# One Trainium2 core, a transformer block in split float32: the gate and up weights in seven products that PSUM adds up, in an order written out for three engines

## The chip, the core and the metric

The kernel runs on one core of a Trainium2 chip. The metric is device time in microseconds. Three runs of the kernel before took 774.23 to 774.93 us, median 774.81. The engines are TensorE (PE in the profile, PEld for its weight loads), VectorE (DVE), ScalarE (ACT), GpSimd (POOL) and SyncE (SP), whose queue issues the loads from memory.

## The reference

One layer of a streaming encoder on 512 tokens of width 1024: a mixer of two attention groups, cross-attention into 256 memory tokens, and a feed-forward part (FFN). The change lies in the last:

```
g, u = jnp.split(h @ w_gate_up, 2, axis=-1)
return (jax.nn.silu(g) * u) @ w_down
```

`w_gate_up` is 1024 x 5632 (gate and up, 2816 columns each), `w_down` is 2816 x 1024. All is float32.

## The kernel before, in words

**Split arithmetic.** Each float32 operand is split into a rounded high part (a copy on ACT) and the rest as a low part (a subtraction on DVE); a product of 128 x 128 weights is three matmuls, high by high, high by low, low by high.

**FFN up, in 22 blocks.** The hidden columns come in eleven units u of 256. Block 2u is the gate's 256 columns of a unit, block 2u+1 the up's. The input `h` lies transposed in `bt`: b11, b21 for tokens 0 to 255 (lower and upper half of the 1024 rows), b12, b22 for tokens 256 to 511. The result of a block is 256 columns by 512 tokens. Blocks 0 and 1 (unit 0) are multiplied plainly in L1078-1088, with weights prepared earlier.

A block is a 2 x 2 by 2 x 2 matrix product, and has two forms. In the plain one (`eight`, L1111) it takes eight products of quarters. In the other (`seven`, L1149) it takes seven products by the scheme of Strassen and Winograd, with sums of quarters of the weights (L951-954, four DVE additions of 128 x 512 a block) and sums of quarters of the input, t1 to t4, which are made once (L1129-1144). `product` (L1090) is one such product: 4 x 3 = 12 matmuls of 128 x 256. Blocks 2, 3 and 11 are plain (EIGHT, L970), the other 17 are sevens.

In a seven of the kernel before, the products land in four PSUM banks (tags a, s, t, o) and DVE adds them up: ACT copies the first product to `v` (L1155), then DVE does five additions that read PSUM (L1161, L1162, L1167, L1169, L1171), ACT applies the silu of a gate block (L1176) and DVE multiplies gate by up in an up block (L1181, L1183). `keep` (L1053) splits the hidden unit (L1062 on ACT, L1063 on DVE) or, for units 4 to 9, leaves it for later.

**The weight ring.** `load_raw` (L896) issues a load of 512 KB from SP's queue into one of three raw buffers, two loads a block. A fill (L919-926) copies from a raw buffer or from the sums into `ring_hi` on ACT (L924) and subtracts into `ring_lo` on DVE (L925). A seven has four fills, one of 128 x 512 and three of 128 x 1024. `take` (L1024) fills ahead as far as the slots of the ring are free. The order of the instructions on every engine is set by the framework's scheduler, from the order of the code and its own estimates.

**FFN down.** Twice (two halves of the output columns) eleven units of `w_down`: units 4 to 8 as sevens too (`seven_products`, L1292), with the hidden unit's sums made by `late_seven` (L1211-1226, DVE operations of 128 x 256 to 128 x 1024) and the weights' by L987-1004; the others plainly (`down`, L1272): 24 matmuls of 128 x 512 for all four token tiles. The fills of `w_down` use the same ring (items of the list of `take`).

Of the kernel before, what the change touches and what calls it, by code (L numbers as in the profile page):

```python
# [14 lines left out]
P = 128  # L15
# [21 lines left out]
def hybrid_block_kernel(  # L37
# [624 lines left out]
    with tc.tile_pool(name="cross", bufs=1, reuse_waits="tile") as cp:  # L662
# [231 lines left out]
        raws = [0]  # L894

        def load_raw(w, k0, nkb, c0, ncol):  # L896
            raws[0] += 1
            raw = wp.tile([P, nkb, ncol], F32, tag="raw", name=f"fraw{raws[0]}", bufs=3)
# [15 lines left out]
        items = []  # L914

        def item(at, size, fill):
            items.append((at, at + size, fill))

# [11 lines left out]
        nslot = [0, 0]  # L930

        def single():
            nslot[0] += 1
            return AS_WEIGHTS + 512 * (nslot[0] % 2)

        def double():
            nslot[1] += 1
            return AS_WEIGHTS + 1024 + 1024 * (nslot[1] % 3)

        def seven_weights(n, c0):  # L940
            raw, total = {}, sums[:, n % 2]
            s2, s4, s3, s1 = (total[:, i] for i in range(4))

            def a11():
                raw["lower"] = load_raw(w_gate_up, 0, 4, c0, 256)
                raw["upper"] = load_raw(w_gate_up, 4, 4, c0, 256)
                return raw["lower"][:, :, :P]

            def s2_s4():
                lower, upper = raw["lower"], raw["upper"]  # L950
                dve.tensor_tensor(out=s1, in0=lower[:, :, P:], in1=upper[:, :, P:], op=ALU.add)  # L951
                dve.tensor_tensor(out=s2, in0=s1, in1=lower[:, :, :P], op=ALU.add)
                dve.tensor_tensor(out=s4, in0=s2, in1=upper[:, :, :P], op=ALU.add)
                dve.tensor_tensor(out=s3, in0=lower[:, :, :P], in1=lower[:, :, P:], op=ALU.add)
                return total[:, 0:2]

            two = dict(c=2, k=4, n=P)
            item(at := single(), 512, fill_from(at, dict(k=4, n=P), a11))
            item(at := double(), 1024, fill_from(at, two, s2_s4))
            item(at := double(), 1024, fill_from(at, two, lambda: raw["upper"], "p c k n -> p k c n"))  # L960
            item(at := double(), 1024, fill_from(at, two, lambda: total[:, 2:4]))

        def eight_weights(n, c0):
            for k0 in (0, 4):
                item(
                    at := double(), 1024,
                    fill_from(at, dict(k=4, n=256), lambda k0=k0: load_raw(w_gate_up, k0, 4, c0, 256)),
                )
# [55 lines left out]
        def take(n=1):  # L1024
            first = taken[0]
            taken[0] += n
            while len(ready) < len(items):
                i = len(ready)
                a, b, fill = items[i]
                if any(j >= first and a < items[j][1] and items[j][0] < b for j in range(max(0, i - 8), i)):  # L1030
                    break
                ready.append(fill())
            return ready[first : first + n]

        take(0)
# [3 lines left out]
        gh, gl, gf = [], [], []  # L1039

        def hidden(u):
# [3 lines left out]
            if u < 4 or u == 10:  # L1045
                return U.rearrange("p t b n -> p b t n")
            if u in (4, 8):
                tag, size = {4: ("vm", 4160), 8: ("pt", 2112)}[u]
# [4 lines left out]
        def keep(u, dst):  # L1053
# [13 lines left out]
            for b in range(2):  # L1067
                gh.append(h[:, b])
                gl.append(l[:, b])
# [6 lines left out]

        accs = [(bank("a"), bank("s")) for _ in range(2)]
# [12 lines left out]
        def product(dst, w, b, first=True, last=True, parts=WHOLE):  # L1090
            for k in range(4):
                if k:
                    parts = WHOLE
                pe.matmul(dst, w[0][:, k, :], b[:, 0, k, :], start=first and k == 0, stop=False)  # L1094
                pe.matmul(dst, w[0][:, k, :], b[:, 1, k, :], start=False, stop=False)  # L1095
                for to in parts:
                    pe.matmul(dst[:, to], w[1][:, k, :], b[:, 0, k, to], start=False, stop=last and k == 3)  # L1097

        left, right = slice(0, 256), slice(256, 512)
        b11, b21, b12, b22 = bt[0][:, 0], bt[0][:, 1], bt[1][:, 0], bt[1][:, 1]  # L1100

        def gate_eight(m, acc):
# [333 lines left out]
```

## Time and profile before

| | value |
|---|---|
| median of three runs | 774.81 us |
| span of the profiled execution | 771.6 us |
| PE busy | 755.6 us, 98% of the span |
| DVE busy | 600.3 us, 78% |
| ACT busy | 429.4 us, 56% |
| granted TensorE clock, mean | 0.998 |
| DMA, mean over the span | 104 GB/s |

The span reaches from the first instruction to the last; of the profiled execution the page gives no other time than the span. The median of the runs is 3.2 us above it, which is taken as what lies around the span. A busy PE is a modelled figure, since matmuls overlap; how fast PE goes is better read from the starts of neighbouring matmuls. A name such as ps_a is the PSUM bank group, `fraw` a raw weight buffer, `sums` the sums of quarters, `ring_hi` and `ring_lo` the weight ring, `thi` and `tlo` t1 to t4, `latex`, `latehi`, `latelo` the hidden units that `late_seven` prepares.

### The profile page before, as it was taken

Reading aid. Unit: us, or ns where it says so; the run is one execution under the profiler, and the core shown is the slowest. Engines: PE = TensorE matmul, PEld = TensorE weight load, DVE = VectorE, ACT = ScalarE, POOL = GpSimd, SP = SyncE. Lnnn points to the kernel's source line nnn. Section 1 sums busy time; section 2 is a strip of 40 time slices with the busy share of each in tenths; the row PEclk is TensorE's granted clock in tenths of the full one; section 3 lists DMA queues with packets and bytes.
Section 4 is the critical chain, followed back from the end, with each engine's and each line's share of the span. In section 5 each row is a group of like instructions: output and inputs, shape, how many; then the busy total and the mean of one; then the engine's idle time right before and its main releaser. Section 6 shows DMA issues by size and latency. Waiting matters only on the chain.

```text
span 771.6 us, 12900 instructions
## 1 busy us (share of the span) xinstructions
PE 755.6 (98%) x5012; PEld 677.0 (88%) x5012; DVE 600.3 (78%) x1098; ACT 429.4 (56%) x784; POOL 62.5 (8%) x105
## 2 busy tenths in 40 slices
PE   9999999999999999999999999999999999999996
PEld 9977888887778988877778999999999999898985
DVE  8668889789886688545653779999899998987746
ACT  7558889567874457444553625554444446553421
POOL 1001132100321210000002100000000000000001
PEclk9999999999999999999999999999999999999999
DMA  7522023422313725311340202332433332233312
GB/s 273 139 70 68 28 56 97 123 82 82 109 56 112 267 98 197 120 54 56 131 143 27 83 28 83 110 110 82 138 110 110 110 110 90 102 112 108 106 59 109
DMA packets 60749, 80.05 MB, mean 104 GB/s; under 512 B 2705, under 2 KB 43665, under 8 KB 60689
## 3 DMA queue, kind: packets, MB, share of 16 engines
q1 hardware_dynamic: 59264, 74.49, 29.9%
q0 software_dynamic: 1280, 4.72, 1.7%
q8 instruction: 39, 0.64, 0.3%
q14 instruction: 22, 0.17, 0.1%
q10 hardware_dynamic: 144, 0.02, 0.0%
HBM read 77.13 MB, written 2.10 MB: 103 GB/s over the span
## 4 chain that ended last, share of the span: by engine, by line
PE 79%; DVE 9%; ACT 6%; issue 3%; DMA 2%; POOL 1%; DVEq 0%; POOLq 0%; ACTq 0%
PE ps_a L144 12%; PE ps_a L146 12%; PE ps_a L143 12%; PE ps_a L1094 3%; PE ps_a L1097 3%; PE ps_a L1095 3%; PE ps_s L1097 3%; PE ps_s L1094 3%; PE ps_s L1095 3%; PE ps_s L143 2%; PE ps_s L144 2%; PE ps_s L146 2%; PE ps_t L552 2%; PE ps_o L561 2%; PE ps_s L533 1%
## 5 line engine op out<-in xcount | busy, mean ns | idle before, releaser
L924 ACT CAST ring_hi<-fraw 128x1024 fp32r<-128x1024 f32 (+1 forms) x62 | 57.2, 932 | 61.0 <-DVE fraw L1003 17.0
L126 DVE TENSOR_TENSOR lo<-raw,hi 128x1024 fp32r<-128x1024 f32 x56 | 68.2, 1224 | 20.5 <-ACT hi L125 20.3
L925 DVE TENSOR_TENSOR ring_lo<-fraw,ring_hi 128x1024 fp32r<-128x1024 f32 (+1 forms) x62 | 66.5, 1075 | 17.4 <-ACT ring_hi L924 17.1
L146 PE MATMUL ps_a<-hTh,lo 128*128 128x512 f32 x192 | 76.6, 399 | 0.0
L144 PE MATMUL ps_a<-hTl,hi 128*128 128x512 f32 x192 | 75.9, 395 | 0.0
L143 PE MATMUL ps_a<-hTh,hi 128*128 128x512 f32 x192 | 75.8, 395 | 0.0
L125 ACT CAST hi<-raw 128x1024 fp32r<-128x1024 f32 x56 | 57.8, 1048 | 25.3 <-PE ps_a L144 21.2
L924 ACT CAST ring_hi<-sums 128x1024 fp32r<-128x1024 f32 x34 | 35.7, 1049 | 35.5 <-PE ps_t L1095 10.2
L925 DVE TENSOR_TENSOR ring_lo<-sums,ring_hi 128x1024 fp32r<-128x1024 f32 x34 | 41.4, 1219 | 2.1 <-ACT ring_hi L924 2.1
L144 PEld LDWEIGHTS ps_a<-hTl,hi 128*128 128x128 f32 x192 | 36.1, 188 | 6.4
L146 PEld LDWEIGHTS ps_a<-hTh,lo 128*128 128x128 f32 x192 | 36.1, 188 | 6.3
L143 PEld LDWEIGHTS ps_a<-hTh,hi 128*128 128x128 f32 x192 | 36.2, 188 | 5.7
L547 ACT ACTIVATE p<-p,nm 128x128 f32<-128x128 f32 (+1 forms) x64 | 36.1, 565 | 8.1 <-DVE nm L537 7.2
L1094 PE MATMUL ps_a<-b,ring_hi 128*128 128x256 f32 x140 | 39.1, 279 | 0.0
L1097 PE MATMUL ps_a<-b,ring_lo 128*128 128x256 f32 (+1 forms) x146 | 39.0, 274 | 0.0
L1095 PE MATMUL ps_a<-b,ring_hi 128*128 128x256 f32 x140 | 38.7, 276 | 0.0
L1097 PE MATMUL ps_s<-b,ring_lo 128*128 128x256 f32 x128 | 35.3, 276 | 0.0
L1095 PE MATMUL ps_s<-b,ring_hi 128*128 128x256 f32 x128 | 35.3, 276 | 0.0
L1094 PE MATMUL ps_s<-b,ring_hi 128*128 128x256 f32 x128 | 35.3, 276 | 0.0
L554 ACT CAST pth<-ps_t 128x128 fp32r<-128x128 f32 (+1 forms) x64 | 27.0, 424 | 14.5 <-PE ps_t L552 13.7
L555 DVE TENSOR_TENSOR ptl<-ps_t,pth 128x128 fp32r<-128x128 f32 (+1 forms) x64 | 30.7, 487 | 5.0 <-ACT pth L554 3.8
L552 PE MATMUL ps_t<-ident,p 128*128 128x128 f32 x160 | 28.1, 275 | 1.1 <-DVE p L549 0.8
(552 smaller groups left out, 2630.5 us busy)
## 6 DMA issues: line engine op xcount, KB each, us to landing
raw<-in_dram SPq DMA_DIRECT2D x64, 512.0 KB, 3.7
fraw<-in_dram SPq DMA_DIRECT2D x62, 512.0 KB, 3.5
cb<-in_dram SPq DMA_DIRECT2D x8, 256.0 KB, 2.5
xo<-in_dram POOLq DMA_DIRECT2D x4, 512.0 KB, 7.5
out_dram<-yd SPq DMA_DIRECT2D x8, 256.0 KB, 2.0
rawv<-in_dram SPq DMA_DIRECT2D x3, 520.0 KB, 6.5
xt<-in_dram SPq DMA_DIRECT2D x3, 512.0 KB, 6.6
gb<-in_dram POOLq DMA_DIRECT2D x3, 512.0 KB, 4.4
```

The costliest lines, as they stand in the source:

```text
L125: act.copy(hi[:, j : j + n, :], raw)
L126: dve.tensor_tensor(out=lo[:, j : j + n, :], in0=raw, in1=f32(hi[:, j : j + n, :]), op=ALU.subtract)
L143: pe.matmul(dst, sh, mh, start=first, stop=False)
L144: pe.matmul(dst, sh, ml, start=False, stop=False)
L146: pe.matmul(dst[:, to], sl, mh[:, to], start=False, stop=last)
L547: act.activation(p[:, :n], p[:, :n], AF.Exp, bias=nm, scale=-1.0, accum_out=sm)
L552: pe.transpose(tp[:, k * P : (k + 1) * P], p[:, k * P : (k + 1) * P], ident)
L924: act.copy(h2, v)
L925: dve.tensor_tensor(out=l2, in0=v, in1=f32(h2), op=ALU.subtract)
L1094: pe.matmul(dst, w[0][:, k, :], b[:, 0, k, :], start=first and k == 0, stop=False)
L1095: pe.matmul(dst, w[0][:, k, :], b[:, 1, k, :], start=False, stop=False)
L1097: pe.matmul(dst[:, to], w[1][:, k, :], b[:, 0, k, to], start=False, stop=last and k == 3)
```

## The change

Six things are changed, all in the FFN's gate and up part.

1. **More sevens.** Block 2 alone is plain; blocks 3 to 21, nineteen of them, are sevens.
2. **PSUM adds up.** A block has three banks: `x`, `p45` and `p2`. Product 1 goes into `x`; ACT copies it out to `early[0]`; product 6 is added on top of it in PSUM; ACT copies that to `early[1]`; product 7 is added on top; ACT copies that to `u3`. Products 4 and 5 go into the two halves of `p45`, and product 3 is added on product 5. DVE then needs one addition of 128 x 512 (`op1`: both halves of `p45` plus `u3`, before product 3 is added) and two of 128 x 256 (`op2`).
3. **Order by hand.** From block 3 to 21 the order on PE, DVE and ACT is the order of the code (`own_order`). On PE a block n is p1, p2, p4, p6, p5, then p3 of block n-1, then p7. The last additions of a block (`op2`) and the gate-by-up product come two blocks later.
4. **Raw weights.** `load_block` loads a block's two halves at the start of block n-2, into five places in turn (three raw buffers and two in `more_room`).
5. **t1 to t4** are made before unit 0's matmuls in the code, no longer after.
6. **Into the down part.** Block 21's p3 is issued after the second token tile of the first down unit, and with it the last `op2` and product of unit 10; ring slots that block 21 still reads are `held` against `take`. The hidden units 1 to 3 lie in the large buffer of units 4 to 7.

```diff
-        EIGHT = (2, 3, 11)
-        for n in range(2, FB):
-            (eight_weights if n in EIGHT else seven_weights)(n, (n % 2) * FF + (n // 2) * 256)
+        SEVENS = range(3, FB)
...
+            if places and w is w_gate_up:
+                raw = places[raws[0] % len(places)].rearrange("p (k n) -> p k n", k=nkb)
...
-            product(p17[:, left], a11, b11, parts=parts)
-            act.copy(v, p17[:, left])
...
-            dve.tensor_tensor(out=O[:, 0], in0=halves(p26), in1=twice(v), op=ALU.add)
-            dve.tensor_tensor(out=O[:, 1, 0], in0=p35[:, left], in1=O[:, 0, 1], op=ALU.add)
...
-            dve.tensor_tensor(out=O[:, 1, 1], in0=p17[:, right], in1=O[:, 0, 1], op=ALU.add)
...
-            dve.tensor_tensor(out=O[:, 0, 1], in0=p4[:, left], in1=O[:, 1, 1], op=ALU.add)
...
-            dve.tensor_tensor(out=O[:, 1], in0=twice(p4[:, right]), in1=O[:, 1], op=ALU.add)
...
+            def p6(self):
+                h, l = ring[self.n, "21"]
+                product(self.x[:, left], (h[:, 0], l[:, 0]), t2, first=False, more=True)
...
+            def op1(self):
+                dve.tensor_tensor(out=self.O[:, :, 1], in0=halves(self.p45), in1=twice(self.u3), op=ALU.add)
+
+            def op2(self):
+                dve.tensor_tensor(out=self.O[:, 0, 0], in0=self.p2[:, left], in1=self.early[:, 0], op=ALU.add)
+                dve.tensor_tensor(out=self.O[:, 1, 0], in0=self.p45[:, right], in1=self.early[:, 1], op=ALU.add)
...
+        own_order = tc.manual_schedule(
+            engines={mybir.EngineType.PE, mybir.EngineType.DVE, mybir.EngineType.Activation}
+        )
+        with own_order:
+            for n in SEVENS:
+                final = n == SEVENS[-1]
+                cur = blocks[n] = Seven(n)
+                one, two = blocks.get(n - 1), blocks.get(n - 2)
+                if n + 2 < FB:
+                    load_block(n + 2)
+                if one:
+                    one.copy_u3()
+                if two:
+                    two.op2()
+                    if not two.gate:
+                        two.mult(0)
+                fill_43(n)
+                if two and two.gate:
+                    two.silu(0)
+                cur.p1()
+                cur.copy_early(0)
+                if one:
+                    one.op1()
+                    if not one.gate:
+                        one.mult(1)
+                if two and not two.gate:
+                    keep(two.u, two.dst)
+                if not final:
+                    sums_21(n + 1)
+                    fill_l0(n + 1)
...
+                if one and one.gate:
+                    one.silu(1)
+                cur.p24()
+                if not final:
+                    fill_u(n + 1)
...
+                cur.p6()
+                cur.copy_early(1)
+                cur.p5()
+                if not final:
+                    sums_34(n + 1)
+                    fill_21(n + 1)
+                else:
+                    fill_last(n)
+                if one:
+                    one.p3()
+                cur.p7()
...
+                    if held and t == 1:
+                        cur.p3()
+                        held.clear()
+                        cur.op2()
+                        cur.mult(0)
+                        keep(cur.u, cur.dst)
```

**DVE, one block in the middle.** Before, an up block (its U is the sum, gf the hidden unit), from its first addition:

```order
L1161 TENSOR_TENSOR U<-ps_s_6118,v 128x512
L1162 TENSOR_TENSOR U<-ps_t_6119,U 128x256
L925 TENSOR_TENSOR ring_lo<-fraw_6126,ring_hi 128x4x2x128
L1167 TENSOR_TENSOR U<-ps_s_6117,U 128x256
L1169 TENSOR_TENSOR U<-ps_t_6120,U 128x256
L1171 TENSOR_TENSOR U<-ps_t_6120,U 128x512
L925 TENSOR_TENSOR ring_lo<-sums,ring_hi 128x1024
L1181 TENSOR_TENSOR gf_5664<-G,U 128x512
L1183 SCALAR_TENSOR_TENSOR gf_5664<-G,U 128x512
```

Now the twelve DVE instructions of a whole block n (here n is odd; the first three finish block n-2, an up block, and L1209 is `op1` of block n-1):

```order
L1212 TENSOR_TENSOR U<-ps_a_5631,U 128x256
L1213 TENSOR_TENSOR U<-ps_s_5630,U 128x256
L1220 TENSOR_TENSOR gf_4979<-G,U 128x512
L923 TENSOR_TENSOR ring_lo<-sums,ring_hi 128x1024
L1209 TENSOR_TENSOR G<-ps_s_5744,v 128x2x256
L944 TENSOR_TENSOR sums<-more_room,place_4642 128x512
L945 TENSOR_TENSOR sums<-sums,more_room 128x512
L923 TENSOR_TENSOR ring_lo<-more_room,ring_hi 128x512
L923 TENSOR_TENSOR ring_lo<-place_4642,ring_hi 128x4x2x128
L949 TENSOR_TENSOR sums<-more_room 128x512
L950 TENSOR_TENSOR sums<-sums,place_4642 128x512
L923 TENSOR_TENSOR ring_lo<-sums,ring_hi 128x1024
```

Five additions out of PSUM became three, and the four fills and four sums that stand here are those of the next block (the first fill, of sums 3 and 4, belongs to blocks n and n-1).

**DVE, unit 0, where t1 to t4 are made.** Before (L1139-1142 are the sums of the input, L1125 the product of gate and up of unit 0, L1135 the low parts of the t's), after the second L887, which writes the low part of b22:

```order
L887 TENSOR_TENSOR b_4280<-f_4578,b_4280 128x1024
L953 TENSOR_TENSOR sums<-sums,fraw_4916 128x512
L1139 TENSOR_TENSOR f_4578<-f_4578,f_4577 128x1024
L954 TENSOR_TENSOR sums<-fraw_4914 128x512
L1125 TENSOR_TENSOR G<-G,ps_s_4637 128x512
```

Now, ahead of that same L887 and behind it (L1102 are the first sums of the input, L181 evacuates the transposed input):

```order
L950 TENSOR_TENSOR sums<-sums,fraw_4632 128x512
L1102 TENSOR_TENSOR f_4579<-b_4279 128x1024
L1102 TENSOR_TENSOR f_4580<-b_4279 128x1024
L181 TENSOR_SCALAR f_4578<-ps_t_4599,gn 128x256
L181 TENSOR_SCALAR f_4578<-ps_t_4608,gn 128x256 x2
L887 TENSOR_TENSOR b_4280<-f_4578,b_4280 128x1024
L1103 TENSOR_TENSOR f_4578<-f_4578,f_4577 128x1024
L1104 TENSOR_TENSOR f_4577<-f_4579,f_4577 128x1024
```

The two L1102 (L1138 before) stood behind unit 0's L1125 and now stand ahead of the L887.

**DVE at the end of gate and up, the last block's `op1`** (L1209; L923 from `sums` is the last fill of gate and up, L1302 and L1306-1309 are `late_seven`, L1212 and L1213 are `op2` of block 20):

```order
L923 TENSOR_TENSOR ring_lo<-sums,ring_hi 128x512
L1212 TENSOR_TENSOR G<-ps_a_6848,rrow 128x256
L1307 TENSOR_TENSOR gf_4979<-gf_4979 128x256
L1302 TENSOR_TENSOR latehi<-gf_4979,latehi 128x256
L1213 TENSOR_TENSOR G<-ps_s_6847,rrow 128x256
L1308 TENSOR_TENSOR gf_4979<-gf_4979 128x256
L1302 TENSOR_TENSOR latehi<-gf_4979,latehi 128x512
L1309 TENSOR_TENSOR gf_4979<-gf_4979 128x256
L1306 TENSOR_TENSOR gf_4979<-gf_4979 128x256
L1302 TENSOR_TENSOR latelo<-gf_4979,latelo 128x256
L1307 TENSOR_TENSOR gf_4979<-gf_4979 128x256
L1209 TENSOR_TENSOR U<-ps_s_6956,v 128x2x256
```

Before, the same place, the last additions of block 21:

```order
L1167 TENSOR_TENSOR U<-ps_s_7032,U 128x256
L925 TENSOR_TENSOR ring_lo<-fraw_7162,ring_hi 128x1024
L1169 TENSOR_TENSOR U<-ps_t_7035,U 128x256
L1223 TENSOR_TENSOR gf_5664<-gf_5664 128x256
L1171 TENSOR_TENSOR U<-ps_t_7035,U 128x512
L925 TENSOR_TENSOR ring_lo<-fraw_7154,ring_hi 128x1024
L1181 TENSOR_TENSOR U<-G,U 128x2x256
L1183 SCALAR_TENSOR_TENSOR U<-G,U 128x2x256
```

Now `late_seven` begins inside block 21, and PE's p3 of block 21 stands behind twelve matmuls of the down part and waits for the L1209 at the end of the first list.

More of the change, by code (lines that the diff above doesn't have):

```diff
@@ L928, in fill_from @@
             return fill
[L930 to L961, printed above, removed]
@@ L975, in hybrid_block_kernel, with fill_eight, item @@
+        def fill_eight(n):
+            for k0, at in ((0, AT_21), (1, AT_43)):
+                ring[n, k0] = fill_from(at, dict(k=4, n=256), lambda: raw_of[n][k0])()
+        SEVENS = range(3, FB)
+        items, held = [], []
+        def item(at, size, fill):
+            items.append((at, at + size, fill))
         SEVEN = (4, 5, 6, 7, 8)
@@ L1088, in hybrid_block_kernel, with product @@
                         )
-        def product(dst, w, b, first=True, last=True, parts=WHOLE):
+        def product(dst, w, b, first=True, last=True, parts=WHOLE, more=False):
             for k in range(4):
```

217 lines of the change are left out of this document (132 added, 85 removed).

## The prediction

> **What bounds the kernel now.** I read the page's busy line first, then the table of windows over the FFN, PE's waits, and PE's timeline. The window rows give the stretch, its length, and busy time with instruction count for PE, PEld, DVE, ACT and POOL, then PE's clock, DMA's share and GB/s. 442 to 649 us is gate and up; 680 to 690 is a piece of the down part.
>
> ```profile
> span 771.6 us, 12900 instructions
> PE 755.6 (98%) x5012; PEld 677.0 (88%) x5012; DVE 600.3 (78%) x1098; ACT 429.4 (56%) x784; POOL 62.5 (8%) x105
> 442.00:649.00 207.00, 207.00 (x1824) 206.92 (x1823) 190.95 (x270) 99.50 (x148) 0.00 (x0) 1.00 0.31 98
> 680.00:690.00 10.00, 8.95 (x76) 8.56 (x75) 8.97 (x16) 5.22 (x7) 0.00 (x0) 1.00 0.18 58
> ```
>
> In gate and up PE is never idle, at a granted clock of 1.00. DVE is 92% busy there, but nothing waits for it. So time in this stage is a number of matmuls times PE's pace. In the down part PE has small holes. PE's timeline gives the pace and the holes (start, duration, and in brackets the idle time before it and what ended it):
>
> ```profile
> 469.81 0.28 PE L1094 MATMUL ps_s<-b,ring_hi 128*128 128x256 f32 x1
> 475.48 0.28 PE L1097 MATMUL ps_s<-b,ring_lo 128*128 128x256 f32 x1
> 667.78 0.39 PE L146 MATMUL ps_a<-ring_hi,g 128*128 128x512 f32 x1
> 670.50 0.39 PE L146 MATMUL ps_o<-ring_hi,g 128*128 128x512 f32 x1
> ```
>
> The first two rows lie 50 matmuls apart: 5.67 / 50 = 0.1134 us for 256 columns. The last two lie 12 apart: 2.72 / 12 = 0.2267 us for 512 columns. A product of 12 matmuls takes 1.36 us, a seven 7 x 1.36 = 9.53 us, and a pair of sevens (gate and up) 19.06 us.
>
> ```profile
> 648.94 0.40 PE L143 MATMUL ps_a<-ring_hi,g 128*128 128x512 f32 x1
> 682.42 0.28 PE L143 MATMUL ps_s<-ring_hi,latehi 128*128 128x256 f32 x1
> 683.10 0.38 PE L144 MATMUL ps_s<-ring_lo,latehi 128*128 128x256 f32 x1 [0.41 <-DVE ring_lo L925]
> 683.32 0.28 PE L146 MATMUL ps_s<-ring_hi,latehi 128*128 128x256 f32 x1
> 687.87 0.28 PE L143 MATMUL ps_s<-ring_hi,latelo 128*128 128x256 f32 x1
> 688.79 0.39 PE L144 MATMUL ps_s<-ring_lo,latelo 128*128 128x256 f32 x1 [0.65 <-DVE ring_lo L925]
> 689.02 0.28 PE L146 MATMUL ps_s<-ring_hi,latelo 128*128 128x256 f32 x1
> 681.82 1.22 DVE L925 TENSOR_TENSOR ring_lo<-fraw,ring_hi 128x1024 fp32r<-128x1024 f32 x1
> 687.51 1.23 DVE L925 TENSOR_TENSOR ring_lo<-fraw,ring_hi 128x1024 fp32r<-128x1024 f32 x1
> ```
>
> 648.94 is the first matmul of the down part. Twice in it PE waits for the low half of a weight slot, until DVE's L925 ends (681.82 + 1.22 = 683.04, and 688.74). By starts, the two holes cost (0.90 - 0.227) + (1.15 - 0.227) = 1.60 us; by the modelled idle times 0.41 + 0.65 = 1.06 us. I take the starts, which do not use modelled ends.
>
> **The change part by part.** The sum is made on the profiled execution, whose span is 771.6 us; the median of the runs lies 3.2 us above it, which stays.
>
> *Fewer matmuls.* Blocks 3 and 11 become sevens: 84 matmuls for 96 each. In PE's order there are 24 fewer matmuls of 128 x 256, and the number of stepped ones is the same. 24 x 0.1134 = **-2.72 us**, all of it on the path, since PE sets the pace there.
>
> *Does the written-out order hold PE's pace?* That hangs on DVE first. Its rows, as neighbours, give the start-to-start time for each width:
>
> ```profile
> 597.11 0.69 DVE L925 TENSOR_TENSOR ring_lo<-fraw,ring_hi 128x512 fp32r<-128x512 f32 x1
> 597.71 0.69 DVE L951 TENSOR_TENSOR sums<-fraw,fraw 128x512 f32<-128x512 f32 x1
> 599.51 1.22 DVE L925 TENSOR_TENSOR ring_lo<-sums,ring_hi 128x1024 fp32r<-128x1024 f32 x1
> 600.65 0.69 DVE L1161 TENSOR_TENSOR G<-ps_a,v 128x512 f32<-128x512 f32 x1
> 601.85 0.42 DVE L1162 TENSOR_TENSOR G<-ps_a,G 128x256 f32<-128x256 f32 x1
> 602.18 1.22 DVE L925 TENSOR_TENSOR ring_lo<-fraw,ring_hi 128x1024 fp32r<-128x1024 f32 x1
> 588.52 0.69 DVE L952 TENSOR_TENSOR sums<-sums,fraw 128x512 f32<-128x512 f32 x1
> 589.25 0.69 DVE L953 TENSOR_TENSOR sums<-sums,fraw 128x512 f32<-128x512 f32 x1
> 585.18 0.62 ACT L924 CAST ring_hi<-fraw 128x512 fp32r<-128x512 f32 x1 [0.24 <-DMA fraw<-in_dram]
> 586.33 0.35 ACT L1155 COPY v<-ps_s 128x256 f32<-128x256 f32 x1
> 586.58 1.05 ACT L924 CAST ring_hi<-sums 128x1024 fp32r<-128x1024 f32 x1
> fraw<-in_dram SPq DMA_DIRECT2D x62, 512.0 KB, 3.5
> ```
>
> 0.60 us for 512 columns, 1.14 for 1024, 0.33 for 256; an addition that needs the one before it takes 0.73 in place of 0.60. A pair of blocks before had six operations of 256 (1.98), sixteen of 512 (9.60), six of 1024 (6.84), and some 0.5 of dependence: 18.9 us. Now it has four of 256 (1.32), fourteen of 512 (two `op1`, eight sums, two fills, two multiplies; 8.40), the six of 1024 and the 0.5: 17.1 us. Against PE's 19.06 DVE has 2 us over in a pair; where `keep` stands in the pair (1.14), 0.9.
>
> A sum is not an order, so I set one block of 9.53 us down by hand, with p1 from 0, p2 from 1.36, p4 2.72, p6 4.08, p5 5.45, p3 of the block before 6.81, p7 8.17. On ACT: `copy_u3` 0.1 to 0.4, `fill_43` (1024) to 1.35, silu to 2.0, `copy_early` of p1 to 2.35. p6 needs that at 4.08: 1.7 us of margin. `copy_early` of p6 waits behind `fill_u`, which starts when p4 has left its slot (4.1), and ends near 5.9; p7 needs it at 8.17. On DVE: low part of `fill_43` 1.4 to 2.55 (p3 needs it at 6.81), `op1` to 3.15 (p3 too), then the sums, `fill_l0`, `fill_u`, two more sums and the low part of `fill_21` to 9.3 at the latest; that one waits for p5 to leave its slot and is needed by p6 4 us into the next block. `op2` ends about 0.4 into the next block; the bank that it frees is needed by p4 at 2.7, a margin of 2, or 1.2 behind a `keep`. No margin is below 1 us; cost in the steady blocks **0**. The raw loads are issued two blocks, 19 us, ahead and land in 3.5 us (last row): 0. The first one into `more_room` goes once unit 0 has left it, near 456, and lands near 461, 4 us ahead of need.
>
> On the three products in one bank, the Trainium skill speaks against this change: "Perfetto Trace Analysis", section Matmuls, says that independent matmul groups should rotate through PSUM banks so that the evacuation of one overlaps the next group. Here product 6 may not start before ACT has copied product 1 out of its bank; by the rule that copy would stand uncovered, and by the rows above it is 0.35 us long with two products (2.72 us) of other banks ahead of product 6. The rival "uncovered copies" below prices it.
>
> *Unit 0, ahead of the blocks.* The low parts of the input's second half (L887, b12 and then b22) are what PE just finds ready:
>
> ```profile
> 439.29 0.48 DVE L181 TENSOR_SCALAR f<-ps_t,gn 128x256 f32<-128x256 f32 x1 [1.42 <-ACT b L179]
> 440.41 0.87 DVE L181 TENSOR_SCALAR f<-ps_t,gn 128x256 f32<-128x256 f32 x2
> 442.86 1.22 DVE L887 TENSOR_TENSOR b<-f,b 128x1024 fp32r<-128x1024 f32 x1
> 444.12 0.38 PE L144 MATMUL ps_a<-b,gate_w 128*128 128x256 f32 x1
> 446.40 1.22 DVE L887 TENSOR_TENSOR b<-f,b 128x1024 fp32r<-128x1024 f32 x1
> 447.76 0.40 PE L144 MATMUL ps_a<-b,gate_w 128*128 128x256 f32 x2
> ```
>
> b12: L887 ends at 444.08 and PE's L144 reads it at 444.12. In PE's new order 15 matmuls that stood ahead of that L144 no longer do: 444.1 - 1.7 = 442.4. On DVE the four L181 now stand in a row; from 439.29, at 0.4 each, and L887: 442.1. b22: L887 ended at 447.62, and the second of the two L144 at 447.76 reads it. In PE's new order 19 more matmuls stand ahead of that one: 447.9 + 2.2 = 450.1. On DVE, behind b12's L887 (its successor can start at 442.0), stand four sums of 512, four L181, two L1102 of 1024 and L887: 442.0 + 2.4 + 1.6 + 2.3 + 1.2 = 449.5. Margins of 0.3 and 0.6 us are thinner than I can work out. Bounds: 0, and one operation of 1024 late, +1.1. I take **+0.2**, near the lower end, since both lists end in time. The t1 to t4 made there come long before block 3 needs one.
>
> *The end of gate and up.* Product 3 of block 21 now stands behind twelve matmuls of 512 columns (2.72 us), 12.25 us after its block's start, and waits for `op1` of block 21. Ahead of that `op1` stand nine DVE operations of 256 columns and one of 512 (9 x 0.33 + 0.60 = 3.6 us) that start near 8.15: the last fill waits until p5 leaves its slot at 6.81, then ACT takes 0.62 and DVE 0.69 for it. 8.15 + 3.6 + 0.69 for `op1` itself is 12.45, 0.2 late. Bounds 0, if the additions that need no late result go ahead of that fill, and +0.8, with one more operation of 512; I take **+0.2**.
>
> *The two holes of the down part.* There DVE is late. From 648.94 to the end of the L925 that ends the first hole DVE took 34.1 us. Now `late_seven` begins inside block 21, where DVE has no next block to prepare. From that `op1`, which starts 2.2 us after the last p7, to the same fill stand 27 operations of 256 columns, 13 of 512 and 11 of 1024: 27 x 0.335 + 13 x 0.60 + 11 x 1.135 = 29.3, so 31.5 us. PE reaches the matmul at 33.7 (682.65, where it would have started without the hole, less 648.94) plus the 1.36 of p3, which moved there: 35.1. The lead is 3.6 us, about 2 if DVE waits for ACT on the way, and by the same count a little more at the second hole. Both go: **-1.6**. Bounds: 0, if some wait holds DVE up by over 3 us, and -1.6. Nothing else was late behind these holes.
>
> Sum: -2.72 - 1.60 + 0.2 + 0.2 = -3.9; 774.8 - 3.9 = **770.9 us**, of which the span is 767.7.
>
> **The rivals.** Under 0.2%, 1.55 us, no measurement of this kernel can be told from no change, so faster means below 773.26 and slower above 776.36.
>
> *Forecast*, 0.62: matmuls and holes. Its own range is 770.5 to 772.4: nothing at the two seams, or +0.8 at one and +1.1 at the other.
>
> *Only the matmuls*, 0.15: the holes stay, or move to another fill, since ring slots are held for block 21 and the order of `late_seven` differs. 774.8 - 2.72 = 772.1. For it: my count leaves out DVE's waits for ACT. Against it: a lead of 2 to 4 us.
>
> *New waits at both seams, and the holes stay*, 0.13: -2.72 + 1.1 (L887 late by one operation of 1024) + 0.5 at block 21 (between its 0.2 and its 0.8) = -1.1, 773.7, within 0.2%. For it: margins of 0.3 and 0.6 us and an `op1` that is late by my own count. Against it: it needs all three at once.
>
> *The written-out order paces the blocks*, 0.10 with its extreme, and slower. Its place is DVE's chain: `fill_43` waits for p7 to leave its slot, and all that stands behind it (`op1`, sums, three fills) waits with it. It decides once DVE needs over 19.06 us a pair, 12% above my 17.1. Then PE waits in every pair; at 0.6 us, one operation of 512, 9.5 pairs are +5.7: 774.8 - 2.72 + 5.7 = 777.8, with the holes staying. For it: DVE is the busiest engine after PE. Against it: each margin in the hand-made block is over 1 us. The extreme is *uncovered copies*, 0.02 of the 0.10: two of 0.35 us in each of 19 blocks are +13.3, 785.4. That the blocks are not what the code says can be excluded: PE's order has the 24 fewer.
>
> **How the numbers follow.** The likeliest case gives 770.9. The range goes from 769.8 (the forecast without seam costs is 770.5; 0.7 below it, half a product, for margins worked out from rows of two decimals over a whole stage) to 774.4 (new waits at both seams at their upper ends: 774.8 - 2.72 + 1.1 + 0.8 is 774.0, and 0.4 over it). It leaves out the slower case and some of the rest. Faster 0.62 + 0.15 = 0.77, same 0.13, slower 0.10.
>
> **What the profile after would show.** 24 fewer matmuls; PE without a wait between 455 and the last p7, and starts at 0.1134: right on the steady blocks. PE waiting at p6 or p7 for ACT, or at p4 or p3 for DVE, in every pair: the slower rival. PE idle near 450 before a matmul that reads b22, ended by L887: the first seam; p3 of block 21 ended by L1209: the second. In the down part no wait of PE for L923 at the two seven matmuls with `latehi` and `latelo`: the holes are gone. I am wrong if PE's busy stretch in gate and up is not shorter, or if holes of over 1 us appear there.

## The result, and the profile after

| | before | after |
|---|---|---|
| median of the runs side by side | 774.87 us | 769.96 us (769.24 to 770.32) |
| medians of a second set, in which before stood twice | 774.76 us (21 runs) and 774.42 us (11 runs) | 769.31 us (5 runs) |
| span of the profiled execution | 771.6 us | 767.5 us |
| time of that execution | 771.6 + 1.74 = 773.3 us | 769.24 us |

The changed kernel is faster: ratio 0.9926, 95% interval 0.9906 to 0.9945, in the second set 0.9923 (0.9911 to 0.9936). That ratio is 5.7 us of 774.8, where 3.9 was forecast. It is not the quotient of the two medians: these lie 4.9 us apart in the first set and 5.5 in the second (774.76 less 769.31). Every run comes with its span and lies 1.7 to 1.8 us above it, in both kernels; so the execution of before that the first profile shows took 773.3 us, less than any of the runs that were listed beside it. From profile to profile the change is 4.1 us, close to the forecast's 3.9. The experiments below ask what other executions of the kernel before lose beyond that. In 51 runs beside the experiments it took 773.06 to 776.65 us; the changed kernel's nine took 768.93 to 770.32.

From the page of the changed kernel, and its window over the piece of the down part:

```profile
span 767.5 us, 12862 instructions
PE 752.7 (98%) x4988; PEld 674.4 (88%) x4988; DVE 595.7 (78%) x1083; ACT 442.9 (58%) x811; POOL 63.6 (8%) x105
680.00:690.00 10.00, 10.00 (x91) 10.00 (x90) 8.14 (x12) 5.11 (x6) 0.00 (x0) 1.00 0.44 143
```

There are 5012 - 4988 = 24 fewer matmuls. In 680 to 690 PE has 91 where it had 76, and no idle time. PE's timeline, before: first matmul of unit 0, first of the down part (648.94, in the prediction), last of all.

```profile
427.68 0.28 PE L143 MATMUL ps_a<-b,gate_w 128*128 128x256 f32 x1
764.12 0.28 PE L146 MATMUL ps_a<-ring_hi,g 128*128 128x256 f32 x1
```

After, the same, with the seams and the places of the two holes:

```profile
427.99 0.28 PE L143 MATMUL ps_a<-b,gate_w 128*128 128x256 f32 x1
438.61 0.88 PE L170 MATMUL ps_t<-ident,y 128*128 128x128 f32 x6 [0.17 <-DVE y L161]
441.36 1.06 PE L170 MATMUL ps_t<-ident,y 128*128 128x128 f32 x8 [0.15 <-DVE f L181]
450.86 0.28 PE L1128 MATMUL ps_a<-b,ring_hi 128*128 128x256 f32 x1
451.07 0.38 PE L144 MATMUL ps_a<-b,gate_w 128*128 128x256 f32 x1
645.33 0.40 PE L143 MATMUL ps_a<-ring_hi,g 128*128 128x512 f32 x1
647.85 0.39 PE L146 MATMUL ps_a<-ring_hi,g 128*128 128x512 f32 x1
648.07 0.28 PE L1127 MATMUL ps_s<-b,ring_hi 128*128 128x256 f32 x1
680.19 0.28 PE L143 MATMUL ps_s<-ring_hi,latehi 128*128 128x256 f32 x1
680.30 0.28 PE L144 MATMUL ps_s<-ring_lo,latehi 128*128 128x256 f32 x1
685.06 0.28 PE L144 MATMUL ps_s<-ring_lo,latelo 128*128 128x256 f32 x1
759.99 0.28 PE L146 MATMUL ps_a<-ring_hi,g 128*128 128x256 f32 x1
```

The DVE rows that these wait for, or would:

```profile
441.64 1.23 DVE L887 TENSOR_TENSOR b<-f,b 128x1024 fp32r<-128x1024 f32 x1
449.79 1.22 DVE L887 TENSOR_TENSOR b<-f,b 128x1024 fp32r<-128x1024 f32 x1
647.19 0.68 DVE L1209 TENSOR_TENSOR U<-ps_s,v 128x512 f32<-128x512 f32 x1
677.26 1.22 DVE L923 TENSOR_TENSOR ring_lo<-fraw,ring_hi 128x1024 fp32r<-128x1024 f32 x1
682.25 1.23 DVE L923 TENSOR_TENSOR ring_lo<-fraw,ring_hi 128x1024 fp32r<-128x1024 f32 x1
```

Gate and up, from the first row to the down part: 221.26 us before, 217.34 after, -3.92. Product 3 of block 21 has left it (1.36) and two products are gone (2.72): -4.08, so 0.16 us was lost. The b22 seam is in it: L887 ends at 451.01, 450.86 to 451.07 is 0.21 where 0.11 is the pace, and the step behind it is 0.22 (to 451.29): 0.2 us. The two runs of transposes wait 0.17 and 0.15 for DVE. Product 3 starts at 648.07, one step behind the matmul ahead of it: `op1` had ended at 647.87. At the first hole the fill ends at 678.48, 1.8 us ahead of the matmul at 680.30; at the second 683.48, 1.6 ahead.

The down part, from its first matmul to the last, takes 114.66 us with product 3 in it, 113.30 without, against 115.18 before: -1.88. So the two stages gained 4.4 us and not 4.1: their first row stands 0.3 us later in the profile after, and that start differs from execution to execution (427.57 us in a second profile of before, 428.44 in no_own_order below).

### The profile page after: what moved, and what is told of

Same layout as the page of the kernel before. It is cut to its first block, busy times and chain, and to the rows that moved or that the text cites. A ratio compares the mean times of both kernels' runs of the same rounds, so it can differ in the third digit from the quotient of the medians.

```text
span 767.5 us, 12862 instructions
## 1 busy us (share of the span) xinstructions
PE 752.7 (98%) x4988; PEld 674.4 (88%) x4988; DVE 595.7 (78%) x1083; ACT 442.9 (58%) x811; POOL 63.6 (8%) x105
## 4 chain that ended last, share of the span: by engine, by line
PE 87%; ACT 6%; DVE 4%; issue 2%; POOL 1%; DMA 1%; DVEq 0%; POOLq 0%; ACTq 0%
PE ps_a L144 13%; PE ps_a L146 13%; PE ps_a L143 13%; PE ps_t L1130 3%; PE ps_t L1127 3%; PE ps_s L1128 3%; PE ps_t L1128 3%; PE ps_s L1127 3%; PE ps_s L1130 3%; PE ps_s L143 2%; PE ps_s L146 2%; PE ps_s L144 2%; PE ps_t L552 2%; PE ps_o L561 2%; PE ps_s L533 1%
## 5 line engine op out<-in xcount | busy, mean ns | idle before, releaser
L923 DVE TENSOR_TENSOR ring_lo<-sums,ring_hi 128x1024 fp32r<-128x1024 f32 (+1 forms) x39 | 46.7, 1196 | 12.9 <-ACT ring_hi L922 8.5
L922 ACT CAST ring_hi<-sums 128x1024 fp32r<-128x1024 f32 (+1 forms) x39 | 40.1, 1029 | 17.2 <-PE ps_s L1128 15.6
L922 ACT CAST ring_hi<-fraw 128x1024 fp32r<-128x1024 f32 (+1 forms) x26 | 26.7, 1033 | 33.5 <-DVE fraw L1009 13.9
L923 DVE TENSOR_TENSOR ring_lo<-fraw,ring_hi 128x1024 fp32r<-128x1024 f32 (+1 forms) x26 | 31.0, 1201 | 14.2 <-ACT ring_hi L922 14.0
L549 DVE TENSOR_SCALAR p<-p,rc 128x128 f32<-128x128 f32 (+1 forms) x64 | 26.8, 418 | 0.1
L552 PEld LDWEIGHTS ps_t<-ident,p 128*128 128x128 f32 x160 | 19.3, 140 | 7.3 <-issue 2.4
L143 PE MATMUL ps_a<-hi,oh 128*128 128x512 f32 x64 | 25.5, 399 | 0.0
L1130 PE MATMUL ps_a<-b,ring_lo 128*128 128x256 f32 (+1 forms) x93 | 25.5, 276 | 0.0
L1127 PE MATMUL ps_a<-b,ring_hi 128*128 128x256 f32 x92 | 25.5, 277 | 0.0
L1128 PE MATMUL ps_a<-b,ring_hi 128*128 128x256 f32 x92 | 25.4, 276 | 0.0
```

Of the source, the lines that this page charges most:

```text
L143: pe.matmul(dst, sh, mh, start=first, stop=False)
L552: pe.transpose(tp[:, k * P : (k + 1) * P], p[:, k * P : (k + 1) * P], ident)
L922: act.copy(h2, v)
L923: dve.tensor_tensor(out=l2, in0=v, in1=f32(h2), op=ALU.subtract)
```

## The experiments

Theory A at the start: the gain is the matmuls and the two holes, and all beyond is spread. Theory B: before loses something that its first profile does not show.

### The two kernels again

Both unchanged, in more rounds, each with a new profile.

> The kernel before, unchanged, with a profile of its own. Theory A (the gain is the 24 matmuls, 2.72 us, and the two holes of the down part, 1.6 us; all beyond 4.3 us is spread between executions): ratio 1.000, every run 1.7 to 1.8 us above its span (not 3.2), two waits of PE for the low half of a weight slot near 683 and 689 us again, 1.4 to 1.6 us by starts. Theory B (before loses more than the first profile shows): the holes, or another wait of PE, come to over 2.5 us in this execution.

> The changed kernel, unchanged, in more rounds. Theory A: 4.3 us under the kernel before, ratio 0.9945, and PE without a wait behind 442 us. Theory B: 5 to 6 us under it, ratio 0.9926 or 0.993 as in the first runs.

Measured: 774.42 us, ratio 0.999 (0.9981 to 1.0), and 769.31, 0.9923 (0.9911 to 0.9936). The second profile of before has a span of 772.4 and what the first had not, a wait of PE in the middle of gate and up. PE's timeline there:

```profile
628.14 0.38 PE L1094 MATMUL ps_s<-tlo,ring_hi 128*128 128x256 f32 x1 [1.27 <-ACT v L1155]
```

ACT's timeline at that place:

```profile
626.59 0.62 ACT L924 CAST ring_hi<-fraw 128x512 fp32r<-128x512 f32 x1 [1.28 <-DMA fraw<-in_dram]
627.11 0.72 ACT L1176 ACTIVATE G<-G 128x256 f32<-128x256 f32 x2
627.73 0.35 ACT L1155 COPY v<-ps_s 128x256 f32<-128x256 f32 x1
```

ACT stands 1.28 us in front of a raw load that has not landed. Behind it in ACT's queue are the silus and then the copy of product 1 to `v`, and PE may not write product 7 into that bank before the copy has read it. In the first profile the same load kept ACT waiting 1.00 us, and PE went on without a wait. With this wait and the two holes the second profile loses 2.9 us by starts, where theory B asked for over 2.5: theory B holds for before. From here on the theories are L, late loads, and D, a DVE that is late by itself.

### The matmuls in the old way

```
-        EIGHT = (2, 3, 11)
+        EIGHT = (2, 3)     # sevens18
+        EIGHT = (2,)       # sevens19
```

> The kernel before with block 11 as a seven, nothing else. Theory A: 12 matmuls of 0.1134 us less, 1.36 us, ratio 0.9982; the holes of the down part stay as they are. Theory B (the sevens alone bring the gain): over 2 us less.

> The kernel before with blocks 3 and 11 as sevens: the change's matmuls in the old way of adding up. Theory A: 24 matmuls less, 2.72 us, if t1 to t4, which are made late here, are ready for block 3; up to 1.5 us of that lost if they are not (a wait of PE near 467 us for the t's); holes stay. Theory B: the five additions out of PSUM make DVE the bound (18.9 us of work in a pair of 19.06) once there is no plain block to catch up in: little gain or a loss, with PE waiting for DVE in the sevens.

Measured: 775.02 us, ratio 1.0003 (0.9994 to 1.0013), and 778.42, 1.0044 (1.0029 to 1.0058). With 12 matmuls less nothing is won, which fits neither theory; with 24 less the kernel is slower, the loss that theory B allowed for. ACT's waits for loads from 465 to 650 us (total, times, longest), one row each from before, before_again, sevens18 and sevens19:

```profile
ACT ring_hi L924 <- DMA fraw<-in_dram: 8.1, 6, 2.7
```
```profile
ACT ring_hi L924 <- DMA fraw<-in_dram: 14.7, 8, 3.9
```
```profile
ACT ring_hi L924 <- DMA fraw<-in_dram: 18.8, 9, 4.9
```
```profile
ACT ring_hi L924 <- DMA fraw<-in_dram: 31.0, 11, 5.6
```

The fewer matmuls PE has, the longer ACT waits for loads in these four. In sevens18 PE waits four times for the copy to `v`, 2.2 us; in sevens19 also for low halves (1.8 us) and for t's at block 3 (0.5).

### Five raw buffers, and three

The change's five buffers in the kernel before, alone and with the sevens:

```
+            if places and w is w_gate_up:
+                raw = places[raws[0] % len(places)].rearrange("p (k n) -> p k n", k=nkb)
...
         keep(0, hidden(0))
+        places += [wp.tile([P, 1024], F32, tag="raw", name=f"place{i}", bufs=3) for i in range(3)]
+        more_room = cp.tile([P, 2176], F32, tag="up", name="more_room")
+        places += [more_room[:, i * 1024 : (i + 1) * 1024] for i in range(2)]
```

> The kernel before, with only the change's five raw buffers (three and two in the place of unit 0's up weights) for the loads of gate and up. Theory L (the time that the kernel before loses from one execution to the next is raw loads that land late: ACT's copy out of a raw buffer waits for them, and the copy of v stands behind it in ACT's queue, on which PE's product in the same bank waits): ACT's waits for loads in gate and up fall from 8 to 15 us to under 3, PE waits for no copy of v, 1 to 1.5 us less (ratio 0.998 to 0.9985) and a smaller spread. Theory D (DVE with 18.9 us of work in 19.06 is late by itself): no change, 774.7.

> The kernel before with the five raw buffers and block 11 as a seven (block 3 stays plain, so no product waits for a late t). If DVE's five additions out of PSUM leave room for it: 1.36 us under five_raw, near 770.8. If they don't: PE waits for low halves of weight slots behind block 11, and the time stays at 772 or over, so that the change's three additions are what lets the matmuls count.

> The kernel before with blocks 3 and 11 as sevens and the five raw buffers, adding up by DVE as before. Theory L: the loss of sevens19 goes, 771 to 772 us (774.7 less 1.4 for the loads less 2.7 for the matmuls, plus about 1 for t's that block 3 waits for). Theory D: stays near 778, PE waiting for DVE's low halves.

Measured: five_raw 772.17 us, ratio 0.9964 (0.9949 to 0.9978); sevens18_five 770.22, 0.9952 (0.9938 to 0.9965); sevens19_five 774.19, 0.9992 (0.9983 to 1.0001). Five buffers alone bring 2.8 us, where theory L had expected 1 to 1.5. ACT's waits for loads fall from 8.1 to 2.0 us, and both holes of the down part are gone. The longer of ACT's two remaining waits in five_raw, 465 to 650 us (the other is 0.2):

```profile
ACT ring_hi L927 <- DMA place<-in_dram: 1.8, 1, 1.8
```

From its DVE and PE timelines, the fill at the end of gate and up, the down part's first matmul, the fill at the place of the first hole, the matmul that reads it, and the last matmul:

```profile
648.62 1.23 DVE L928 TENSOR_TENSOR ring_lo<-fraw,ring_hi 128x1024 fp32r<-128x1024 f32 x1
648.94 0.40 PE L143 MATMUL ps_a<-ring_hi,g 128*128 128x512 f32 x1
679.96 1.22 DVE L928 TENSOR_TENSOR ring_lo<-fraw,ring_hi 128x1024 fp32r<-128x1024 f32 x1
682.52 0.28 PE L144 MATMUL ps_s<-ring_lo,latehi 128*128 128x256 f32 x1
762.22 0.28 PE L146 MATMUL ps_a<-ring_hi,g 128*128 128x256 f32 x1
```

Before, the same fill at the end of gate and up, ACT's part and DVE's:

```profile
649.38 2.00 ACT L924 CAST ring_hi<-fraw 128x1024 fp32r<-128x1024 f32 x2 [2.03 <-DMA fraw<-in_dram]
650.47 1.23 DVE L925 TENSOR_TENSOR ring_lo<-fraw,ring_hi 128x1024 fp32r<-128x1024 f32 x1 [1.43 <-ACT ring_hi L924]
```

A late load held ACT, ACT held DVE for 1.43 us, and DVE carried that to the holes 33 us later. With five buffers the same fill starts 1.85 us earlier, and so does the fill at the first hole: 679.96 against 681.82, 1.86 us. It ends 1.3 us ahead of PE's matmul. The down part takes 762.22 - 648.94 = 113.28 us against 115.18: the holes cost 1.90.

With the buffers, block 11 as a seven is worth what its matmuls say: sevens18_five ends gate and up 1.27 us sooner than five_raw (219.75 us against 221.02 from the first matmul of unit 0). So DVE's five additions left room for that, and theory D falls for it. Block 3 does not pay in the old order, and 774.19 is the number of neither theory: PE waits 0.85 us there for t's, then for low halves, and a hole stands in the down part again. How much of that is the t's and how much DVE, these runs don't part.

In the changed kernel, three buffers in place of five, in two ways:

```
-        places += [more_room[:, i * 1024 : (i + 1) * 1024] for i in range(2)]   # three_raw and three_raw_late
...
-                if n + 2 < FB:
-                    load_block(n + 2)
+                if n + 1 < FB:                                                   # three_raw_late
+                    load_block(n + 1)
```

> The changed kernel with three raw buffers in place of five. Theory L: the loads land late again, ACT waits for them in every block and PE behind it: 3 to 15 us more, 772 to 784. Theory D (what carries is the lighter DVE): within 0.5 us of the changed kernel, 769.3 to 769.8.

> The changed kernel with three raw buffers, each block's loads issued one block ahead. The second load of a block can go when the last sum of the block before has read its buffer, about 8 us into the block before that, and lands 3.5 us later, 2 us into a block; ACT's fill wants it at 2.4, DVE's first sum at 3.2. If the five buffers are needed in the new order too: waits of ACT for loads, 1 to 5 us more, 770.5 to 774. If the new order reads late enough: within 0.5 us, 769.3 to 769.8, with hardly a wait of PE.

three_raw writes the loads two blocks ahead into buffers whose contents are still to be read, so part of its blocks work with the weights of a later block; its 770.27 us (0.9936, 0.9923 to 0.9949) says little on lateness. three_raw_late reads the right weights in every block: 769.42, ratio 0.9941 (0.9929 to 0.9954) beside runs of before with a median of 774.37, and its trace ends where the changed kernel's does:

```profile
760.00 0.28 PE L146 MATMUL ps_a<-ring_hi,g 128*128 128x256 f32 x1
```

ACT waits for no load there between 465 and 650 us. So three buffers do in the new order; the old order needed the two more. That it is the later reading and the earlier freeing of the buffers that makes the difference, and not the lighter DVE, is the likely reason and was not tested apart.

### Without the written-out order

```
-        with own_order:
+        if True:
```

> The changed kernel without the written-out order: the scheduler orders the same instructions from block 3 to 21. If the written-out order is part of the gain: 2 to 8 us more, with waits of PE for ACT's copies between the products of one bank. If the lighter DVE and the early loads do it: within 1 us of the changed kernel.

Measured: 770.0 us, ratio 0.9935 (0.9922 to 0.9948), PE without a wait in the blocks. The scheduler put PE's matmuls of the blocks in the same order as the written-out one; what changed is the order on DVE and ACT. By the medians that order is worth 0.7 us at the most, and the intervals of the two ratios overlap. What another order on PE would cost, this run does not show.

### Filling DVE up

```
+            for _ in range(2):                            # dve_plus1; range(3) in dve_plus2
-            dve.tensor_tensor(out=s1, in0=lower[:, :, P:], in1=upper[:, :, P:], op=ALU.add)
+                dve.tensor_tensor(out=s1, in0=lower[:, :, P:], in1=upper[:, :, P:], op=ALU.add)
...
-                parts = IN_STEP if self.gate and self.u in (2, 4, 6, 8, 10) else WHOLE
+                parts = IN_STEP if self.gate and self.u in (2, 4, 6, 8, 10) or self.n in (9, 10, 11) else WHOLE  # plus1_step
```

> The changed kernel with the first sum of each block (128 x 512 on DVE) made twice. By the prediction's count DVE goes from 17.1 to 18.3 us in a pair of 19.06: no wait of PE in the blocks, within 0.4 us of the changed kernel (769.3 in the runs so far), up to 1 us more only in the pairs with keep. If DVE is the hidden bound: 5 us more or over.

> The same sum made three times: 19.5 us in a pair of 19.06, 20.6 where keep stands. By the count PE now waits for DVE in every pair, 0.4 to 1.5 us, 4 to 8 us more in all, 773 to 777. If DVE had more room than counted: no change.

> dve_plus1 with the stepped product (its first low matmul in two halves) also in blocks 9, 10 and 11. Theory S (a wait of 0.06 us of PE in block 8 put its matmuls to 0.1178 us each in place of 0.1133, until the next stepped product 40 us later in block 12): the slow stretch ends at block 9, 521 us, about 1.2 us less than dve_plus1, so 1.2 us nearer to the changed kernel, less 0.06 for each step. Rival (the pace is slower because DVE is busy without a pause there): 0.1178 goes on through blocks 9 to 11, and the time stays that of dve_plus1.

Measured: dve_plus1 771.66 us, ratio 0.9962 (0.9947 to 0.9977); dve_plus2 780.7, 1.0083 (1.0067 to 1.0098); plus1_step 770.65, 0.9957 (0.9945 to 0.997). The threshold lies near where the count put it: dve_plus1, 0.8 us under it in a pair, has no wait of over 0.1 us in the blocks. Above it the price is higher than expected: dve_plus2 loses 11.4 us against the changed kernel, where 4 to 8 stood. In dve_plus2 PE waits at product 4 for `op2`, in its place in the prediction's rival (PE, then DVE):

```profile
537.24 0.28 PE L1131 MATMUL ps_a<-b,ring_lo 128*128 128x256 f32 x1
538.83 0.39 PE L1128 MATMUL ps_s<-tlo,ring_hi 128*128 128x256 f32 x1 [1.31 <-DVE G L1214]
538.36 0.41 DVE L1214 TENSOR_TENSOR G<-ps_s,rrow 128x256 f32<-128x256 f32 x1
```

dve_plus1 is 2.3 us slower all the same, where 0.4, or 1 with the pairs that hold `keep`, was expected. The windows 513 to 555, of dve_plus1, the changed kernel and plus1_step:

```profile
513.00:555.00 42.00, 42.00 (x360) 42.00 (x359) 41.30 (x59) 23.52 (x37) 0.00 (x0) 1.00 0.39 122
```
```profile
513.00:555.00 42.00, 42.00 (x373) 42.00 (x372) 39.15 (x54) 24.10 (x38) 0.00 (x0) 1.00 0.37 118
```
```profile
513.00:555.00 42.00, 41.94 (x369) 41.74 (x368) 41.55 (x59) 23.34 (x37) 0.00 (x0) 1.00 0.39 124
```

In dve_plus1 PE is busy throughout, but gets through 360 instructions in place of 373: 13 x 0.1134 = 1.5 us. (Another 0.3 is a wait at product 3 of block 21; the rest of the 2.3 was not traced.) Where the slower stretch begins in dve_plus1, PE's and DVE's timelines:

```profile
515.07 0.33 PE L1128 MATMUL ps_s<-tlo,ring_hi 128*128 128x256 f32 x1
515.24 0.28 PE L1129 MATMUL ps_s<-tlo,ring_hi 128*128 128x256 f32 x1
547.04 0.28 PE L1129 MATMUL ps_t<-thi,ring_hi 128*128 128x256 f32 x1
514.55 0.41 DVE L1214 TENSOR_TENSOR G<-ps_s,rrow 128x256 f32<-128x256 f32 x1
```

`op2` ends at 514.96, and product 4 starts at 515.07 with one step of 0.17 in place of 0.11. From there PE goes at 0.1178 us a matmul (515.24 to 547.04 are 270 of them) until the stepped product of block 12.

plus1_step was meant to end that stretch at block 9. By the medians it is 1.0 us faster than dve_plus1, where 1.2 was expected, but it does not show that the steps did it. The same place in its trace, product 4 of block 8 and the first of the added steps:

```profile
514.82 0.28 PE L1129 MATMUL ps_s<-tlo,ring_hi 128*128 128x256 f32 x1
521.75 0.33 PE L1131 MATMUL ps_t<-b,ring_lo 128*128 128x128 f32 x2
```

These are 61 matmuls apart, 6.93 / 61 = 0.1136 us: behind a wait of 0.05 us this execution kept the faster pace, before any added step was reached. So the run leaves open whether a step ends the slower pace; in dve_plus1 it did end at one, that of block 12. What the run does show is that a busy DVE does not make the slower pace: DVE is busy for 41.55 of the 42 us here, and PE gets through 369 instructions (three of them added halves).

### The copies bare

```
+                cur.p6()
+                cur.copy_early(1)
                 cur.p24()
...
-                cur.p6()
-                cur.copy_early(1)
                 cur.p5()
```

> The changed kernel with product 6 right behind product 1 in the same bank, ahead of products 2 and 4, so that ACT's copy between them has no matmuls to lie under. The prediction priced an uncovered copy at 0.35 us; ACT's queue has a fill and in half of the blocks a silu ahead of it, so 0.4 to 1.0 us in each of 19 blocks: 8 to 19 us more, 777 to 788. Against that: if the copy costs PE nothing either way (another cause covers it), 769 to 770.

Measured: 792.14 us, ratio 1.0228 (1.0213 to 1.0243), 22.8 more than the changed kernel, above the expected 8 to 19. PE, and ACT below it, in one of the 19 blocks:

```profile
562.32 0.39 PE L1127 MATMUL ps_t<-thi,ring_hi 128*128 128x256 f32 x1 [0.71 <-ACT rrow L1184]
560.42 1.06 ACT L922 CAST ring_hi<-sums 128x1024 fp32r<-128x1024 f32 x1
561.38 0.63 ACT L1216 ACTIVATE G<-G 128x512 f32<-128x512 f32 x1
561.90 0.36 ACT L1184 COPY rrow<-ps_t 128x256 f32<-128x256 f32 x1
```

The 19 places take 0.62 to 1.25 us over the pace by starts. In the two places where ACT is free when product 1 ends, it is 0.62: the copy itself, and the last matmul of product 1, which it waits for. In 8 gate blocks, as here, the silu stands ahead of the copy in ACT's queue, 0.88 or 1.00 us in all. In 9 up blocks the copy waits 0.66 us for DVE, whose product of gate and up (L1220) still reads the half of U that it overwrites; these are the dearest, at 1.25 us, and their wait is no matter of the bank. Here the bank rule of the Trainium skill ("Perfetto Trace Analysis", section Matmuls) is seen at work: with the next group in the same bank, the copy is not covered. In the change products 2 and 4, in other banks, cover it.

### Product 3 of block 21 at its place

```
             cur.op1()
+            cur.p3()
             cur.mult(1)
```

(and its call in the down part taken out).

> The changed kernel with product 3 of the last block at the end of gate and up, no longer behind the first two token tiles of the down part. op1 of that block ended 2.5 us after the last product 7 in the changed kernel: PE waits for it, 2.0 to 2.6 us more, 771.3 to 772. If DVE runs the late op1 earlier there: under 1 us.

Measured: 769.8 us, ratio 0.9938 (0.9922 to 0.9955). The edit did not do what it was for: PE still has ten matmuls of the down part ahead of product 3.

```profile
645.86 0.40 PE L143 MATMUL ps_a<-ring_hi,g 128*128 128x512 f32 x1
647.93 0.39 PE L143 MATMUL ps_a<-ring_hi,g 128*128 128x512 f32 x1
648.46 0.38 PE L1127 MATMUL ps_s<-b,ring_hi 128*128 128x256 f32 x1
```

The last step is 0.53 where 0.23 is the pace: two matmuls less of cover cost 0.3 us. The price without any cover was not measured.

## Why the prediction was right and wrong

**Right, by its own steps.** The 24 matmuls are worth 2.72 us once nothing else is late: gate and up is shorter by them and by product 3 to within 0.16 us. The steady blocks cost nothing, and the threshold on DVE stands near where the prediction had put it. Both holes go. From profile to profile the sum was -3.9 and 4.1 was measured; that this is so close is in part luck, since the two stages gained 4.4 and an earlier stage, which the sum leaves out, gave 0.3 back.

**Too low: the price of a bare copy.** The rival "uncovered copies" took 0.35 us for each. In copy_bare the copy takes 0.36, but a place costs 0.62 to 1.25, since the copy starts only when product 1 has ended, ACT is free and, in an up block, DVE has read what it overwrites.

**Wrong: the base.** "The median of the runs lies 3.2 us above it, which stays." 1.74 us lies around the span; the other 1.5 was that this execution of before was a fast one. The profiled execution of the changed kernel was less so: the medians lie 0.7 us above it in the first set (769.96 against 769.24) and 0.1 in the second. So of the 1.5 most did not stay. Part of what the fast execution had been spared is late loads: five_raw takes 2.8 us off the median, and only 1.9 off this profile.

**Wrong: "The raw loads ...: 0."** That step priced the loads of the new order, rightly, and did not ask what the old loads cost. ACT's waits for loads were there to be read in the first profile (8.1 us in gate and up), and behind them in ACT's queue the copy to `v` on which PE depends. five_raw measures this term: 2.8 us, of which 1.9 are the two holes, which the sum had, at 1.6, for another reason. In the first profile only the holes were visible.

**Right in sign, with another cause: the holes.** The prediction laid them on DVE's amount of work and on `late_seven` beginning earlier. five_raw leaves both as they were, and the holes go: the fill comes 1.86 us sooner, of which 1.43 are DVE's wait behind a late load at the end of gate and up. Whether the lighter DVE would have closed them without that is not shown. The lead at the first hole is 1.8 us, where the count gave 3.6, "about 2 if DVE waits for ACT". The price by starts, 1.60, was short by 0.3, which the slower pace behind the second hole explains (64 matmuls at 0.1177 in place of 0.1134). The 682.65 of the count is one matmul too late: without the hole PE's matmul starts at 682.53, and in five_raw it does at 682.52.

**The seams.** +0.4 was taken for both. The head lost 0.16 net. By starts, b22 cost 0.2, as was taken, and the transposes, which the prediction had not named, some 0.35 more than before; against that, before had itself lost some 0.3 there, with a wait of 0.1 at b12 and 52 matmuls at 0.1178 behind it, which this execution of the changed kernel did not have. `op1` of block 21 came 0.2 us ahead of need and not 0.2 behind it, since the last fill started 0.3 us earlier than counted: it goes into the half of the slot that product 6 reads, and so did not wait for product 5 (ACT began it at 642.12, and product 5 ran to 642.6). Had these two come to 0.2 together, and the loads counted at five_raw's 2.8 in place of the holes' 1.6, the sum would be 774.8 - 2.7 - 2.8 + 0.2 = 769.5.

**Open.** Why the same loads land late in one execution and not in another is not shown. That late loads are all that spreads the executions of before is not shown either: only two of them were profiled. Nor is the split, in block 3 under the old order, between late t's and DVE.

## What to carry to other kernels

One profile is one execution: compare its time with the spread of the runs first, and where it is among the fastest, look for waits off the critical path that a slightly worse execution would put on it. A late load is read behind the engine that waits for it: what stands next in that queue, and who waits for that. Taking work away from the bound engine pays only when its suppliers can follow, so price the supply at the new pace; here 12 matmuls less were worth nothing with three buffers in the old order, and their full price with five.

## What the runs showed of the hardware

At a granted clock of 1.00 PE's matmuls of 128 x 256 followed one another at one of two paces, 0.1133 or 0.1178 us from start to start. In dve_plus1 the slower pace set in behind a wait of 0.06 us and lasted some 37 us, to a product whose first low matmul is issued in two halves. It also lay behind the second hole of before, where the low matmuls are 0.35 us apart in place of 0.34 (three matmuls):

```profile
689.61 0.28 PE L144 MATMUL ps_t<-ring_lo,latelo 128*128 128x256 f32 x1
691.73 0.28 PE L144 MATMUL ps_s<-ring_lo,latev 128*128 128x256 f32 x1
```

(six steps, 2.12 / 18 = 0.1178). Not every wait is followed by it. Behind the first hole of before the pace is 4.55 / 40 = 0.1137 (683.32 to 687.87 in the prediction's rows), and none of the 19 waits of copy_bare, 0.62 to 1.25 us, was followed by the slower one. So a wait can cost more than its idle time; what decides whether it does is not shown.
